# Gate product zs stored raw in a gated attention and gMLP block: silu and factors taken in later pairs, query parts laid out row by row

## The chip, the cores and the metric

The kernel runs on one core of a Trainium2 chip. The metric is the device time of one execution in microseconds (us); the time of a kernel is the median of several executions.

## The reference

One layer of a streaming encoder over 1024 tokens of width 1024, all in float32. Cut to what the change touches:

```python
h = rmsnorm(x, norm_g)
q, k, v, za, u, vs, zs, gm = split(h @ w_in)          # columns of one projection
q, k = partial_rope(q, pos), partial_rope(k, pos)     # first 16 of 64 dims of each head
a = window_sink_attention(q, k, v, sinks)             # 16 heads, 2 key heads, chunks of 64
a = (a * silu(za)) @ w_att_out
sgo = chunked_spatial_gating(gelu(u), gelu(vs), ...)  # called s1 in the kernel
sgo = (sgo * silu(zs)) @ w_sg_out
ga, gs = split(sigmoid(gm + b_merge))
y = ga * a + gs * sgo
out = rmsnorm(x + y @ w_o, final_g)
```

The output has to hold `silu(zs) * s1` in front of `w_sg_out`, wherever silu and product are taken.

## The kernel before, in words

**Pairs.** Every 1024x1024 projection is made in four *pairs* of 128-row blocks (`m` = 0, 2, 4, 6). A pair is one call of `gemm_pair` (L350): seven products by a Strassen-like scheme instead of eight. A product (L333) is 12 matmuls of 128x512, since each float32 operand is split into a high and a low float32r part (`split`, L148: ScalarE casts the high part, VectorE subtracts it from the source) and three of the four partial products are kept, over four blocks of depth. The seven products come in the order b11, t1, t2, b21, t3, b22, t4, by the names of the seven forms of the right operand (tiles `T_b11h`, `T_b11l` and so on, one buffer each). Between the products stand ScalarE copies out of PSUM (L359, L363, L366), VectorE adds (L371, L376, L380), four calls of `finish`, one for each quarter of the pair's result, and a `hook` after each product. The quarter tiles come from a ring of five (`xtile`, L95), the PSUM banks from rings of two per name (`bank`, L83).

**Weights.** `split_next` (L208) splits one weight tile at four places of a pair (tiles `wh`, `wl`, rings of three); the tiles come from DRAM on SyncE's queue one pair ahead. The engines work through their instructions in order; the order of the program is set by a scheduling layer from the order in which the code is written, dependencies, and the explicit ones that `after` (L158) adds.

**Stages.** In this order: head and vs; four pairs of u with the spatial mixing, which writes `s1_dr` (L789); the pair of keys and values; four pairs of q; four pairs of zs; four of gs and four of ga (both merge gates, stored raw by `rest`, L464); four of za; four of `w_sg_out`; four of `w_att_out`; the last projection. The attention runs beside the zs pairs from `m` = 2 on and beside gs and ga: each hook there takes one or two *parts* of the generator `attention` (`part_of_attention`, L1255, nine parts for a pair, one for a hook in the first pair): scores and exponentials (`softmax_stage`, L1097), transposes of the weights (`weight_stage`, L1151), values (`value_stage`, L1183).

**The q pairs.** `finish` (L984) stores a quarter raw to `q_raw` and, scaled and split, to `q_hl`, shape (2, 1024, 1024), high part first (`split_q`, L883, store at L894). The rotary rows go through `rotate` (L937): loads of `q_raw` on SyncE's queue (L943, tiles `rot`), six VectorE operations (L963 to L970), and `split_q` again. `rotate(1, 1)` falls into the first zs pair. `query_stage` (L1032) loads 64x4x128 blocks of `q_hl` for the attention (L1038).

**The zs pairs.** `zs_pair` (L1052) collects the four quarters. When the pair's products are issued, it takes the silu of all four on ScalarE (L1069), after the latest sink exponential (L1138), then multiplies each by its quarter of `s1_dr` on VectorE (L1079) and stores it to `s_dr` (L1080). The factors are loaded by `get` (L459): in the first pair into `rot` tiles after the products, later two of them ahead, into two buffers `g`.

**The za pairs.** `finish` (L1367) takes silu of the quarter, multiplies it by a quarter of `at_dr`, the attention's result (tiles `g`, four buffers, a pair ahead), and stores `a_dr`. From `m` = 2 on, `part_of_loads` loads the four quarters of `s_dr` (`bq`, 128x4x512, 1 MB each, four buffers, L1286). `forms_of` (L1327) makes the seven forms of the next right operand from them, b11 to t4, on ScalarE and VectorE (L155, L156, L185).

## Time and profile before

| what | value |
|---|---|
| time, three runs | 929.25, 927.65, 929.3 us; median 929.25 |
| the profiled execution's own time | 928.08 us |
| its span, first to last instruction | 926.3 us, 1.78 us less |
| mean granted TensorE clock | 0.996 |
| busy TensorE (PE) | 908.1 us, 98% |
| busy VectorE (DVE), ScalarE (ACT), GpSimd (POOL) | 689.6, 529.5, 126.9 us |
| moved by DMA | 201.71 MB, mean 218 GB/s |

Times in the profile count from the start of the span. In a group of instructions stand the line, the engine, the operation, output<-input, shape and count, then busy us and mean ns of one, then the idle time of the engine just before and what ended it. In a timeline a row has start, duration (of the group if several instructions are merged, "x4"), engine, line, operation, and in brackets the idle time ahead of it and its releaser. PE is TensorE's matmul, SPq SyncE's queue of DMA issues. Where matmuls overlap in the records, the distance of two starts is the cost of one: 0.227 us for 128x512. A row of stretches has start:end, length, then busy us and count for PE, PEld (weight loads), DVE, ACT and POOL, then granted clock, share of the DMA engines and GB/s.

### The profile page before, as it was taken

The numbers are of one execution on the slowest core, as the hardware profiler recorded it, in microseconds if no ns is written. First come the engines' busy times: TensorE is split into PE (matmuls) and PEld (weight loads), VectorE is DVE, ScalarE is ACT, GpSimd is POOL, SyncE is SP. The second block draws the span as 40 slices with busy tenths as digits, with TensorE's granted clock in tenths as the row PEclk, the third lists the DMA queues.
The fourth block names the chain that finished last, engine by engine and source line by source line (L and its number), as shares of the span: only waits on it lengthen the run. The fifth ranks groups of instructions, "written<-read, shape, count | busy, mean of one in ns | idle before, by whom it ended". The sixth has DMA issues, their size and how long they took to land.

```text
span 926.3 us, 13212 instructions
## 1 busy us (share of the span) xinstructions
PE 908.1 (98%) x4332; PEld 753.4 (81%) x4332; DVE 689.6 (74%) x1243; ACT 529.5 (57%) x1056; POOL 126.9 (14%) x189
## 2 busy tenths in 40 slices
PE   8999999999999989999999999999999999999996
PEld 5888888888888778888888888888887887888885
DVE  6874776656678678888878888746498589579996
ACT  6862433334444468887766676744475475467443
POOL 0002222213011001101111121001100111210012
PEclk9999999999999999999999999999999999999999
DMA  6327678877788777878787779779658765998632
GB/s 239 137 87 208 212 192 185 167 155 220 238 284 266 214 240 193 220 214 233 188 228 258 234 172 254 213 259 327 214 200 316 266 198 156 295 310 286 205 114 114
DMA packets 128830, 201.71 MB, mean 218 GB/s; under 512 B 12441, under 2 KB 60825, under 8 KB 128762
## 3 DMA queue, kind: packets, MB, share of 16 engines
q1 hardware_dynamic: 109608, 148.17, 48.9%
q0 software_dynamic: 19008, 52.44, 23.7%
q8 instruction: 34, 0.56, 0.2%
q14 instruction: 34, 0.28, 0.1%
q10 hardware_dynamic: 146, 0.27, 0.1%
HBM read 144.07 MB, written 86.11 MB: 249 GB/s over the span
## 4 chain that ended last, share of the span: by engine, by line
PE 83%; DVE 9%; DMA 3%; issue 2%; ACT 2%; SPq 0%; DVEq 0%; ACTq 0%
PE ps_mm L341 34%; PE ps_o L341 25%; PE ps_mm L600 4%; PE ps_sc L1115 3%; PE ps_sc L341 2%; PE ps_tp L341 2%; PE ps_o L1200 2%; PE ps_tp L1159 2%; DVE wl L156 2%; PE ps_tp L772 2%; DVE bq L185 1%; PE ps_tp L569 1%; PE ps_sc L569 1%; PE ps_o L569 1%; PE ps_mm L569 1%
## 5 line engine op out<-in xcount | busy, mean ns | idle before, releaser
L155 ACT CAST wh<-s 128x1024 fp32r<-128x1024 f32 (+1 forms) x78 | 78.2, 1005 | 96.1 <-PE ps_mm L341 43.1
L156 DVE TENSOR_TENSOR wl<-wr,wh 128x1024 fp32r<-128x1024 f32 (+1 forms) x80 | 75.7, 947 | 55.3 <-ACT wh L155 54.6
L155 ACT CAST wh<-wr 128x1024 fp32r<-128x1024 f32 (+1 forms) x80 | 66.3, 830 | 81.8 <-PE ps_mm L341 39.0
L156 DVE TENSOR_TENSOR wl<-s,wh 128x1024 fp32r<-128x1024 f32 (+1 forms) x78 | 90.9, 1166 | 12.1 <-ACT wh L155 12.1
L341 PE MATMUL ps_o<-T_b22h,wh 128*128 128x512 f32 x148 | 59.6, 403 | 2.5 <-ACT x L363 2.5
L341 PE MATMUL ps_o<-T_t1h,wh 128*128 128x512 f32 x148 | 59.3, 400 | 0.3 <-ACT wh L155 0.2
L341 PE MATMUL ps_o<-T_b22l,wh 128*128 128x512 f32 x148 | 58.3, 394 | 0.0
L341 PE MATMUL ps_o<-T_b22h,wl 128*128 128x512 f32 x148 | 58.3, 394 | 0.0
L341 PE MATMUL ps_o<-T_t1h,wl 128*128 128x512 f32 x148 | 57.8, 391 | 0.0
L341 PE MATMUL ps_o<-T_t1l,wh 128*128 128x512 f32 x148 | 57.6, 389 | 0.0
L341 PE MATMUL ps_mm<-T_b11h,wl 128*128 128x512 f32 x140 | 54.8, 392 | 2.0 <-DVE wl L156 2.0
L341 PE MATMUL ps_mm<-T_t4h,wh 128*128 128x512 f32 x140 | 55.2, 394 | 1.5 <-DMA q<-q_hl 0.8
L341 PE MATMUL ps_mm<-T_t2h,wh 128*128 128x512 f32 x140 | 54.9, 392 | 1.2 <-ACT x L359 1.2
L1128 ACT ACTIVATE pr<-ps_sc,sm 128x192 f32<-128x192 f32 (+2 forms) x128 | 50.9, 409 | 8.3 <-DVE sm L1124 7.2
L341 PE MATMUL ps_mm<-T_t3h,wh 128*128 128x512 f32 x140 | 55.2, 395 | 0.0
L341 PE MATMUL ps_mm<-T_b11h,wh 128*128 128x512 f32 x140 | 55.0, 393 | 0.0
L341 PE MATMUL ps_mm<-T_t4h,wl 128*128 128x512 f32 x140 | 54.7, 391 | 0.0
L341 PE MATMUL ps_mm<-T_b11l,wh 128*128 128x512 f32 x140 | 54.7, 390 | 0.0
L341 PE MATMUL ps_mm<-T_t3h,wl 128*128 128x512 f32 x140 | 54.6, 390 | 0.0
L341 PE MATMUL ps_mm<-T_t2h,wl 128*128 128x512 f32 x140 | 54.6, 390 | 0.0
L341 PE MATMUL ps_mm<-T_t2l,wh 128*128 128x512 f32 x140 | 54.5, 390 | 0.0
L341 PE MATMUL ps_mm<-T_t4l,wh 128*128 128x512 f32 x140 | 54.5, 389 | 0.0
(354 smaller groups left out, 2407.8 us busy)
## 6 DMA issues: line engine op xcount, KB each, us to landing
wr<-in_w_dram SPq DMA_DIRECT2D x86, 256.0 KB
sums<-in_w_dram POOLq DMA_DIRECT2D x20, 512.0 KB, 5.7
s<-sums SPq DMA_DIRECT2D x20, 512.0 KB
s_dr<-x SPq DMA_DIRECT2D x32, 256.0 KB
q_hl<-qhl SPq DMA_DIRECT2D x16, 512.0 KB
q<-q_hl SPq DMA_DIRECT2D x64, 128.0 KB
wr<-in_w_dram SPq DMA_DIRECT2D x14, 512.0 KB
y_dr<-x POOLq DMA_DIRECT2D x28, 256.0 KB, 6.6
```

Source lines behind the costliest of these rows:

```text
L155: nc.scalar.copy(hi, src)
L156: return nc.vector.tensor_sub(lo, src, hi.bitcast(F32))
L185: op(dst[:, i : i + 2, :], a[:, i : i + 2, :], c[:, i : i + 2, :])
L341: nc.tensor.matmul(acc, lt, rt, start=fresh and k == 0 and n == 0, stop=k == 3 and n == 2, skip_group_check=True,)
L569: mm = nc.tensor.matmul(acc, lt, rt, start=k == 0 and n == 0, stop=k == KC - 1 and n == 2)
L600: nc.tensor.matmul(acc[:], lt, rt, start=k == 0 and n == 0, stop=k == KC - 1 and n == 2)
L772: nc.tensor.matmul(pm[:, t * P : (t + 1) * P], xh[:, half * 4 + t, g * P : (g + 1) * P], bias[-1][1][:, g % 4, :], start=True, stop=True,)
L1115: nc.tensor.matmul(sc[:, i, k0:], q_of[:, c, i * P : (i + 1) * P], kt[:, f, k0:], start=f == 0, stop=f == 1,)
L1128: nc.scalar.activation(held_in[c, i], sc[:, i, lo:hi], AF.Exp, bias=nmax[:, c, i : i + 1], scale=-1.0, accum_out=sums[:, c, i : i + 1],)
L1159: nc.tensor.transpose(dst, pr[:, i, block * P : block * P + width], ident[:])
L1200: nc.tensor.matmul(po[:, cs], lt, rt, start=n == 0, stop=n == len(terms) - 1)
```

## The change

1. `zs_pair` goes. The zs pairs use `rest` and store the raw quarter to `z_dr` right after each quarter is made: no silu, no factor, no wait for the exponentials.
2. The za pairs get a table of steps by pair and hook (`parts_of_s`): load the quarters of `z_dr` into `bq` tiles (four named buffers now), take silu in them on ScalarE (128x1024 each), load the same quarter of `s1_dr` as factor, and multiply on VectorE (128x1024). The factor uses buffer 0, which the last quarter needs; so that quarter's factor comes in four pieces of 128x512 through tiles `g2` and `g3`.
3. The za pairs' own factors from `at_dr` have two buffers, `g0` and `g1`, instead of four, and are asked for two quarters ahead instead of four.
4. `q_hl` becomes (1024, 2, 2, 512): for each row and half, high and low part beside each other, 4 KB in a piece; a rotated group is stored by two DMAs in place of four.
5. `rotate`'s loads of `q_raw` go to GpSimd's queue.

The diff, cut to its core (`bq(n)` in place of the ring of four and `want_gate` in place of `want_gates` at other places are left out):

```diff
-    q_hl = scratch("q_hl", (2, D, S))
+    q_hl = scratch("q_hl", (D, 2, 2, HALF))
...
         for at, dst in places:
-            nc.sync.dma_start(dst, hl[at].bitcast(F32))
+            nc.sync.dma_start(dst, hl[at].rearrange("p a t -> p (a t)").bitcast(F32))
...
-                nc.sync.dma_start(dst[halves[half]], src[:, :, half_of(half)])
+                nc.gpsimd.dma_start(dst[halves[half]], src[:, :, half_of(half)])
...
-            rows = q_hl[j].rearrange("(c r d) t -> r d c t", r=2, d=HD)[par]
+            rows = q_hl[:, t // 4, j].rearrange("(c r d) t -> r d c t", r=2, d=HD)[par]
...
-    def zs_pair(m, hook, *place, ahead_by=0):
...
-    zs_pair(0, part_of_q, 5, "rot")
+    gemm_pair(hb, rest(z_dr, 0), part_of_q)
...
-        exps.append(nc.scalar.activation(es[:], es[:], AF.Exp))
+        nc.scalar.activation(es[:], es[:], AF.Exp)
...
-    for m in range(2, KC, 2):
-        zs_pair(m, lambda: part_of_attention(m == 2), 2, ahead_by=3)
-    for dst in (gs_dr, ga_dr):
-        for m in range(0, KC, 2):
-            gemm_pair(hb, rest(dst, m), part_of_attention)
+    for dst in (z_dr, gs_dr, ga_dr):
+        for m in range(2 if dst is z_dr else 0, KC, 2):
+            gemm_pair(hb, rest(dst, m), lambda: part_of_attention(dst is z_dr and m == 2))
...
+        def silu(j, half):
+            for c in range(0, 4, 2):
+                v = s_q[j, half][:, c : c + 2, :]
+                nc.scalar.activation(v, v, AF.Silu)
+
+        def multiply(j, half, c):
+            v = s_q[j, half][:, c : c + 2, :]
+            after(nc.vector.tensor_mul(v, v, factors[-1][:, c : c + 2, :]), term[0])
...
+            (0, 1): [(load, 0, 0), (load_factors, 0, 0)],
+            (0, 2): [(load, 0, 1)],
+            (0, 3): [(load, 1, 1)],
+            (0, 5): [(silu, 0, 0)],
+            (0, 6): [(multiply, 0, 0, 0)],
+            (0, 7): [(multiply, 0, 0, 2), (load_factors, 0, 1)],
+            (2, 3): [(silu, 0, 1)],
+            (2, 6): [(multiply, 0, 1, 0)],
+            (2, 7): [(multiply, 0, 1, 2), (load_factors, 1, 1), (silu, 1, 1)],
+            (4, 2): [(multiply, 1, 1, 0), (multiply, 1, 1, 2), (load, 1, 0), (load_last, 0), (load_last, 1)],
+            (4, 6): [(silu, 1, 0)],
+            (4, 7): [(multiply_last, 0), (multiply_last, 1), (load_last, 2), (load_last, 3)],
+            (6, 1): [(multiply_last, 2), (multiply_last, 3)],
...
     for m in range(0, KC, 2):
         if m == 0:
-            want_gates(at_dr, m)
-        if m == 2:
-            s_q = {}
-            ahead_of_time += loads_of_quarters(s_q, s_dr)
+            for _ in range(2):
+                want_gate(at_dr, *of_att.pop(0), 2)
...
-            if m < 6:
-                gates.append(get(at_dr, m + 2 + i, half, 4))
+            if of_att:
+                want_gate(at_dr, *of_att.pop(0), 2)
 
-        gemm_pair(hb, finish, part_of_loads, "tp")
+        gemm_pair(hb, finish, lambda: part_of_s(m), "tp")
```

**Where instructions stand now.** Three places of the two in-order engines that feed TensorE. First VectorE, at the end of the first zs pair and the start of the second, before:

```order
L245 TENSOR_TENSOR s_2588<-wr_2581,s_2587 128x512
L156 TENSOR_TENSOR wl_2721<-s_2587,wh_2720 128x1024
L156 TENSOR_TENSOR wl_2741<-s_2588,wh_2740 128x1024
L1079 TENSOR_TENSOR x_2590<-x_2590,rot_2756 128x512
L1079 TENSOR_TENSOR x_2592<-x_2592,rot_2760 128x512
L1079 TENSOR_TENSOR x_2591<-x_2591,rot_2764 128x512
L1079 TENSOR_TENSOR x_2739<-x_2739,rot_2768 128x512
L156 TENSOR_TENSOR wl_2895<-wr_2582,wh_2894 128x512
L1123 TENSOR_REDUCE sm_2793<-ps_sc_2796 128x2
```

The same place now (L1087 is the first operation of the softmax, L1123 before):

```order
L380 TENSOR_TENSOR x_2587<-x_2587,ps_o_2610 128x512
L156 TENSOR_TENSOR wl_2716<-s_2583,wh_2715 128x1024
L890 SCALAR_TENSOR_TENSOR qhl_2672<-rot_2603,qhl_2672 128x256 x2
L156 TENSOR_TENSOR wl_2738<-s_2584,wh_2737 128x1024
L1087 TENSOR_REDUCE sm_2770<-ps_sc_2773 128x2
L1087 TENSOR_REDUCE sm_2770<-ps_sc_2782 128x2
```

The four products with factors (L1079) no longer stand between the weights' low parts and the first softmax. Second, VectorE a little earlier, in the first zs pair around the rotation of the queries, before:

```order
L371 TENSOR_TENSOR x_2590<-x_2590,ps_o_2656 128x512
L963 TENSOR_TENSOR rot_2608<-rot_2606,tab_306_2068 128x512
L156 TENSOR_TENSOR wl_2671<-wr_2581,wh_2670 128x1024
L964 TENSOR_TENSOR rot_2609<-rot_2607,tab_318_2124 128x512
L969 TENSOR_TENSOR rot_2606<-rot_2606,tab_318_2124 128x512
L965 TENSOR_TENSOR rot_2608<-rot_2608,rot_2609 128x512
L968 TENSOR_TENSOR rot_2607<-rot_2607,tab_306_2068 128x512
L376 TENSOR_TENSOR x_2592<-x_2592,ps_mm_2589 128x512
```

and now:

```order
L960 TENSOR_TENSOR rot_2604<-rot_2602,tab_306_2068 128x512
L371 TENSOR_TENSOR x_2586<-x_2586,ps_o_2650 128x512
L156 TENSOR_TENSOR wl_2666<-wr_2577,wh_2665 128x1024
L961 TENSOR_TENSOR rot_2605<-rot_2603,tab_318_2124 128x512
L966 TENSOR_TENSOR rot_2602<-rot_2602,tab_318_2124 128x512
L962 TENSOR_TENSOR rot_2604<-rot_2604,rot_2605 128x512
L965 TENSOR_TENSOR rot_2603<-rot_2603,tab_306_2068 128x512
L376 TENSOR_TENSOR x_2588<-x_2588,ps_mm_2585 128x512
```

The same eight operations, but L371 now stands behind the first rotation product (L963 before, L960 now). Third, ScalarE in the first za pair, from the copy after product t2 to the copy after b11 of the next pair, before:

```order
L366 COPY x_6316<-ps_mm_6314 128x512
L155 CAST wh_6381<-wr_6293 128x1024
L1368 ACT_TABLE_LOAD
L1368 ACTIVATE x_6315<-x_6315 128x512
L1368 ACTIVATE x_6317<-x_6317 128x512
L155 CAST wh_6421<-s_6295 128x1024
L1368 ACTIVATE x_6316<-x_6316 128x512
L155 CAST wh_6443<-s_6296 128x1024
L1368 ACTIVATE x_6437<-ps_mm_6314 128x512
L359 COPY x_6456<-ps_mm_6455 128x512
```

and now, from the second silu of a quarter of z on (L1349; L1398 is the silu of za, L1368 before):

```order
L1349 ACTIVATE bq_1140_6259<-bq_1140_6259 128x1024
L1398 ACTIVATE x_6245<-x_6245 128x512
L155 CAST wh_6359<-s_6227 128x1024
L1349 ACTIVATE bq_1143_6277<-bq_1143_6277 128x1024
L1398 ACTIVATE x_6244<-x_6244 128x512
L1349 ACTIVATE bq_1143_6277<-bq_1143_6277 128x1024
L1398 ACTIVATE x_6376<-ps_mm_6242 128x512
L155 CAST wh_6382<-s_6228 128x1024
L1349 ACTIVATE bq_1146_6296<-bq_1146_6296 128x1024
L359 COPY x_6398<-ps_mm_6397 128x512
L1349 ACTIVATE bq_1146_6296<-bq_1146_6296 128x1024
```

Of the eight silu on quarters of z, six stand in this one stretch, the first of them just ahead of these rows behind the table load, and five stand ahead of the copy L359; the table of steps has two of the quarters a pair later, the scheduling layer put them here. On SyncE's queue all three quarters and the first factor, 4 MB, are issued in one run between the second and the third of the gates from `at_dr`.

98 lines of the change are left out of this document (51 added, 47 removed).

## The prediction, as put on record before the run

> **What bounds the kernel now.** The head of the page comes first, then TensorE's waits over the whole span (us in total, times, longest):
>
> ```profile
> PE 908.1 (98%) x4332; PEld 753.4 (81%) x4332; DVE 689.6 (74%) x1243; ACT 529.5 (57%) x1056; POOL 126.9 (14%) x189
> ```
>
> ```profile
> PE ps_o L341 <- ACT x L363: 2.5, 1, 2.5
> PE ps_mm L341 <- DVE wl L156: 2.0, 2, 1.1
> ...
> PE ps_mm L341 <- ACT x L359: 1.2, 2, 0.9
> ...
> PE ps_mm L341 <- DVE x L376: 0.7, 1, 0.7
> ```
>
> TensorE is the bound, so only what it loses can be won. Those waits are small, but they don't show how much slower it ran around them. The table of stretches does; first from t1 of the second zs pair to t1 of the first gs pair (four pairs), then four later pairs:
>
> ```profile
> 320.77:432.45 111.68, 107.05 (x556) 88.39 (x556) 91.06 (x215) 85.23 (x228) 11.88 (x14) 0.98 0.80 225
> 458.59:562.00 103.41, 103.41 (x569) 89.29 (x568) 84.15 (x198) 72.59 (x211) 14.10 (x20) 1.00 0.77 222
> ```
>
> The later four run without a gap. Both stretches hold 28 products; by the code the first has 34 parts of attention, the second 36. From the chain, a product takes 2.72 (24 matmuls in 5.44):
>
> ```profile
> 626.62 5.44 PE ps_mm L341 x24
> ```
>
> So 28 products are 76.2, the 36 parts 27.2 or 0.76 each, and the first stretch without its stalls is 103.41 - 2 x 0.76 = 101.9. **It loses 9.8 us**: 4.6 idle (111.68 - 107.05), the rest slower running. The largest piece shows why (timelines of the four engines):
>
> ```profile
> 328.80 0.39 PE L341 MATMUL ps_o<-T_b21h,wl 128*128 128x512 f32 x1
> 331.67 0.80 PE L341 MATMUL ps_o<-T_b22h,wh 128*128 128x512 f32 x1 [2.49 <-ACT x L363]
> ...
> 334.40 0.63 PE L341 MATMUL ps_o<-T_b22h,wh 128*128 128x512 f32 x1
> ```
>
> ```profile
> 314.23 5.13 SPq L894 DMA_DIRECT2D q_hl<-qhl  x8
> ...
> 320.74 1.85 SPq L200 DMA_DIRECT2D rot<-s_dr  x4
> ...
> 328.52 2.50 SPq L457 DMA_DIRECT2D s_dr<-x  x4
> ```
>
> ```profile
> 327.80 0.69 DVE L1079 TENSOR_TENSOR x<-x,rot 128x512 f32<-128x512 f32 x1 [6.79 <-DMA rot<-s_dr]
> ```
>
> ```profile
> 331.02 0.60 ACT L363 ACTIVATE x<-ps_o 128x512 f32<-128x512 f32 x1 [4.12 <-DMA s_dr<-x]
> 331.94 1.28 ACT L1128 ACT_TABLE_LOAD   x1 [0.32 <-DMA s_dr<-x]
> ```
>
> Read it backwards. Product b22 needs L363, which needs one of the five quarter tiles; that is free only when its store is done, and the store waits for the factor, which SyncE issues behind eight stores of `q_hl` (the trace gives the name `s_dr` to loads of `s1_dr` too). VectorE stands 6.79 at the product with the factor. TensorE loses 331.67 - 328.80 - 0.23 = 2.6, and seven matmuls after it cost (334.40 - 331.67) / 6 = 0.46 each instead of 0.23, another 1.6: 4.2 in all.
>
> **The change: zs beside the attention.** These operations leave the four zs pairs:
>
> ```profile
> L1069 ACT ACTIVATE x<-x 128x512 f32<-128x512 f32 x12 | 7.1, 624 | 0.6 <-DVE x L376 0.5
> L1069 ACT ACT_TABLE_LOAD x4 | 5.1, 1283 | 0.1
> L1128 ACT ACT_TABLE_LOAD x4 | 5.1, 1283 | 0.4 <-DMA s_dr<-x 0.3
> ...
> L1079 DVE TENSOR_TENSOR x<-x,g 128x512 f32<-128x512 f32 x12 | 8.2, 690 | 7.3 <-DMA g<-s_dr 3.9 <-ACT x L1069 3.2
> ```
>
> Seven of the eight table loads go (9.0 us of ScalarE), and 16 silu and 16 products. What stays has the same sequence per quarter as gs and ga, whose stretch has no stall, so all 9.8 are to be had. One thing is late next: the first softmax, which now follows TensorE closely. Its scores, then t1 and 9 matmuls of t2, then its transposes: 21 matmuls are 4.8, and the second scores about 1, so 5.8. Before, that chain took
>
> ```profile
> 331.19 0.61 DVE L1123 TENSOR_REDUCE sm<-ps_sc 128x2 f32<-128x128 f32 x2
> ```
>
> ```profile
> 336.55 0.68 PE L1159 MATMUL ps_tp<-ident,pr 128*128 128x128 f32 x4
> ```
>
> 5.4, with a table load in it. The cover is 0.4; ScalarE's L363 and VectorE's weight parts share it. Bounds 0 and 1.5 lost; I take 0.8. **Term: -9.0** (-9.8 to -8.3).
>
> **Rotation in the first zs pair.** The last product of that pair waits for L376:
>
> ```profile
> 305.17 2.56 SPq L943 DMA_DIRECT2D rot<-q_raw  x4
> ```
>
> ```profile
> 309.62 0.69 DVE L963 TENSOR_TENSOR rot<-rot,tab 128x512 f32<-128x512 f32 x1 [0.73 <-DMA rot<-q_raw]
> ...
> 311.61 0.69 DVE L964 TENSOR_TENSOR rot<-rot,tab 128x512 f32<-128x512 f32 x1 [0.16 <-DMA rot<-q_raw]
> ...
> 314.02 0.68 DVE L376 TENSOR_TENSOR x<-x,ps_mm 128x512 f32<-128x512 f32 x1
> ```
>
> This stall (0.7 in the list of waits) does not go: the rotation stays in front of L376. Now L371 (0.6) also waits for the rotation's first load: the rows from 309.62 to 314.02 move down by its 0.6, less the idle 0.16 in them, so L376 comes some 0.4 later. And the four loads come by GpSimd's queue. Not shown before; the nearest rows for that queue (KB each, us from issue to landing):
>
> ```profile
> at_dr<-aT POOLq DMA_DIRECT2D x16, 256.0 KB, 5.4
> ...
> k_dr<-qhl POOLq DMA_DIRECT2D x16, 32.0 KB, 3.3
> ```
>
> Between them for 128 KB; SyncE's took 4.4 to the first rotation (309.62 - 305.17). So 1.1 earlier to 1.0 later; I take no difference, since 4.4 is also the middle of the two rows. Half as many SyncE issues for rotated rows free the queue, nothing waits for that any more. **Term: +0.4** (-0.7 to +1.4).
>
> **The za pairs.** ScalarE gets eight silu of 1024 and VectorE six products of 1024 and four of 512; for their sizes stand a cast and a subtraction, 1.05 and 1.22:
>
> ```profile
> L155 ACT CAST T_b11h<-bq x2: 1050/1052/1053, 670.7 to 671.6; 128x1024 fp32r<-128x1024 f32 x2
> ```
>
> ```profile
> L185 DVE TENSOR_TENSOR bq<-bq,bq 128x1024 f32<-128x1024 f32 x16 | 19.1, 1217 | 0.9 <-DMA bq<-s_dr 0.9
> ```
>
> That is 8.4 and 10.0 us. The room is in the stretches of the first za pair; DVE is the third of the five busy times after the length, ACT the fourth:
>
> ```profile
> 603.00:623.00 20.00, 20.00 (x96) 16.66 (x94) 8.55 (x12) 9.16 (x14) 1.14 (x2) 1.00 0.71 246
> 623.00:643.00 20.00, 20.00 (x89) 16.54 (x89) 12.04 (x16) 8.61 (x13) 2.19 (x4) 1.00 0.99 355
> ```
>
> Both are half idle, so it fits on average. The tight place is the end of the first pair: six silu between 619 and 634, five ahead of L359.
>
> ```profile
> 618.80 0.58 ACT L366 COPY x<-ps_mm 128x512 f32<-128x512 f32 x1
> ...
> 632.10 0.59 ACT L359 COPY x<-ps_mm 128x512 f32<-128x512 f32 x1 [1.36 <-PE ps_mm L341]
> ```
>
> Walking its new order with these durations: table load to 620.7, silu and quarter's silu in turn to 625.2, the weight cast when its buffer is free at 626.5, then three silu of z, two of za, one cast, and L359 ends at 633.3. TensorE needs it for t2 at
>
> ```profile
> 634.78 2.72 PE ps_mm L341 x12
> ```
>
> so 1.4 are left. The last silu ahead of L359 needs quarter (1,1) by 631.7. In front of its end are 0.5 MB of sums, 0.5 of gates and four times 1 MB, 5.2 MB from about 613.3 on: at the 355 GB/s of the lower of these two rows 628.0, at the 246 of the upper 634.6, then late by 2.9, of which 1.4 is covered. I take the higher rate, since a queue with several MB in it is the lower row's case, and 0.2 for the rest. **Term: +0.2** (0 to +1.5).
>
> VectorE's backlog later, when the forms are made, is what the `wl` waits above stand for. The last two products with factors stand ahead of it, in
>
> ```profile
> 671.74 2.36 DVE L156 TENSOR_TENSOR T_b11l<-bq,T_b11h 128x1024 fp32r<-128x1024 f32 x2 [1.56 <-ACT T_b11h L155]
> ```
>
> two times 0.69 in an idle 1.56: nothing, up to 1 if their loads are late. The longer pieces of `q_hl` are hidden: no wait hangs on bytes there.
>
> **Sum.** -9.0 + 0.4 + 0.2 = **-8.4**. The profiled execution took 928.08 (span 926.3 and 1.8 around it), 1.2 below the median shown; it would take 919.7. With the three runs the mean is 928.57, and from there I forecast **920.2**.
>
> **The rivals.** *A, rotation loads late.* GpSimd's issue is held up or its landing slow. For it: nothing but software issue stands there. Against: 3.3 and 5.4 above. If they come 3 later, L376 waits 3 more and TensorE slows after it as at 331.67: 3 + 1.6, so 924.8. In the Trainium skill, "SBUF — State Buffer", section "SBUF: two separate sides", speaks against this edit: while VectorE runs an operation in a two-port mode, GpSimd cannot write the descriptors of its DMAs. By that rule the loads would wait for VectorE, which makes A likelier where such operations run; the trace's k_dr landing of 3.3 beside a working VectorE shows no such hold.
>
> *B, ScalarE waits for z.* At 246 GB/s the first za pair loses 1.5, and the quarters' chain (factor, product, next load into buffer 0) as much again: 923.
>
> *C, the stall only moves.* The first softmax or a quarter tile's store stops TensorE by 2 to 3 as before, and it slows again: 4.2 of the 9.8 stay, 924.4.
>
> *D, slower: gates two quarters ahead.* A gate from `at_dr` is now asked for after the product two places earlier, and VectorE meets it two quarters on, with the weights' low part behind it.
>
> ```profile
> 642.26 0.69 DVE L1369 TENSOR_TENSOR x<-x,g 128x512 f32<-128x512 f32 x1
> ...
> 647.74 0.68 DVE L1369 TENSOR_TENSOR x<-x,g 128x512 f32<-128x512 f32 x1
> ```
>
> That leaves 647.74 - 642.95 = 4.8 to land 256 KB, and TensorE takes the low part about 2 later. A store of that size took 4.75:
>
> ```profile
> 300.35 4.75 DMA q_raw<-x
> ```
>
> so it holds on average. To be slower, the four pairs must lose 10.3 (the 8.4 and 0.2%), 2.6 each: landing 9.4 or more after the issue, every time. Behind the 4 MB that can happen once, not four times. It would give 931.
>
> **Chances.** Forecast 0.62 (917.8 to 922), A 0.12, B 0.14, C 0.05, D 0.07. Faster by over 0.2% of 929.25 (1.9 us, about what a measurement of this kernel can tell from no change) is a time below 927.4: the forecast, A, B and 0.02 of C, together 0.90. Within 0.2% is the rest of C, 0.03, where more of the loss returns than the 4.2 kept there; slower is D, 0.07. The range reaches from the forecast with all bounds good to A and B: 917.8 to 925.5.
>
> **What would show it.** Right: no wait on L363, L359 or `q` between 320 and 432, four pairs in about 102.7; no ACT_TABLE_LOAD at each zs pair any more, only one ahead of the first exponential and one ahead of the first silu of za; L376 at 314 to 315; L359 of the second za pair before 634 by the old clock. Wrong: idle TensorE at the first transposes (C), a `rot` wait over 1.5 on VectorE (A), a ScalarE wait for `bq` (B), a VectorE wait for `g` in every za pair (D).

## The result and the profile after

The changed kernel takes **932.82 us** (median of ten runs, 930.46 to 936.28), the kernel before, beside it, 928.66 (ten runs, 927.65 to 929.3). The ratio is **1.0047** with a 95% interval of 1.0036 to 1.0059: slower, where the forecast was 920.2. The profiled execution of the changed kernel took 931.92 us, its span is 930.1, its mean granted clock 0.992.

The head of the page after:

```profile
PE 908.0 (98%) x4332; PEld 755.4 (81%) x4332; DVE 688.2 (74%) x1237; ACT 519.9 (56%) x1045; POOL 131.7 (14%) x197
```

ScalarE and VectorE have less to do, as forecast, and TensorE the same. The span is 3.8 longer all the same. TensorE's waits over the span (us in total, times, longest) show one new large one:

```profile
PE ps_mm L341 <- DVE x L376: 8.6, 3, 5.0
```

That line had 0.7 in one wait before. To see where the time went, the span is cut at the first matmul of t1 in each pair and each stretch compared with its own before:

| stretch | before | after | difference | forecast |
|---|---|---|---|---|
| pair of keys and values, last 20 us | 20.16 | 20.84 | +0.7 | - |
| first zs pair | 20.94 | 27.75 | **+6.8** | +0.4 |
| the four pairs from the second zs pair to the first gs pair | 111.68 | 102.32 | **-9.4** | -9.0 |
| third za pair | 19.04 | 24.07 | **+5.0** | +0.2 |
| making the forms (second stretch behind it) | 14.90 | 14.90 | 0 | 0 |
| one pair behind 804 | 19.04 | 19.87 | +0.8 | - |

With -0.4 in the head and +0.1 between the ends, that makes +3.7; the spans differ by 3.8. The stretches after; the first two answer to the two of before:

```profile
327.89:430.21 102.32, 102.31 (x556) 87.82 (x556) 81.46 (x201) 72.46 (x215) 11.78 (x14) 1.00 0.70 190
456.39:559.84 103.45, 103.45 (x569) 89.28 (x568) 84.16 (x198) 72.53 (x211) 14.07 (x20) 1.00 0.75 219
648.82:672.89 24.07, 21.01 (x86) 16.75 (x84) 16.57 (x20) 9.52 (x13) 2.15 (x5) 0.93 0.77 270
```

The four pairs now run without a gap at full clock, as the later four do. The third za pair has idle TensorE of 3.1 and a clock of 0.93. So the part of the change that was worked out most closely came true, and two parts that were put down as nearly free cost 11.8.

**The first zs pair after.** Timelines of SyncE's queue, GpSimd, VectorE and TensorE, in that order:

```profile
302.32 0.82 SPq L457 DMA_DIRECT2D q_raw<-x  x1
...
306.34 2.70 SPq L1035 DMA_DIRECT2D q<-q_hl  x4
```

```profile
308.69 1.67 POOL L943 DMA_DIRECT2D rot<-q_raw  x3 [5.91 <-DMA q_raw<-x]
```

```profile
313.26 0.69 DVE L960 TENSOR_TENSOR rot<-rot,tab 128x512 f32<-128x512 f32 x1 [6.36 <-DMA rot<-q_raw]
...
318.44 0.68 DVE L376 TENSOR_TENSOR x<-x,ps_mm 128x512 f32<-128x512 f32 x1
```

```profile
319.17 0.79 PE L341 MATMUL ps_mm<-T_t4h,wh 128*128 128x512 f32 x1 [5.04 <-DVE x L376]
...
323.60 0.63 PE L341 MATMUL ps_mm<-T_t4l,wh 128*128 128x512 f32 x1
```

Three of the four loads are issued at 308.69, when the last store of `q_raw` has landed, some 3 us later than SyncE issued them before (305.17 to 307.73). The four loads of the queries for the attention go out just ahead of them, from 306.34 on. VectorE stands 6.36 at the first rotation, L376 ends at 319.12, and TensorE has lost 5.04. After that the rows are (323.60 - 319.17) / 10 = 0.44 apart instead of 0.23 for a dozen matmuls.

**The third za pair after.** SyncE's queue, VectorE, ScalarE, TensorE:

```profile
650.31 0.37 SPq L200 DMA_DIRECT2D bq<-s_dr  x1
...
662.16 0.37 SPq L200 DMA_DIRECT2D bq<-z_dr  x1
```

```profile
659.77 2.36 DVE L1353 TENSOR_TENSOR bq<-bq,bq 128x1024 f32<-128x1024 f32 x2 [5.48 <-DMA bq<-s_dr]
...
662.65 0.68 DVE L371 TENSOR_TENSOR x<-x,ps_tp 128x512 f32<-128x512 f32 x1
...
664.99 0.68 DVE L376 TENSOR_TENSOR x<-x,ps_mm 128x512 f32<-128x512 f32 x1
```

```profile
667.28 2.01 ACT L1349 ACTIVATE bq<-bq 128x1024 f32<-128x1024 f32 x2 [0.96 <-DMA bq<-z_dr]
```

```profile
665.72 0.74 PE L341 MATMUL ps_mm<-T_t4h,wh 128*128 128x512 f32 x1 [3.06 <-DVE x L376]
...
669.24 0.39 PE L341 MATMUL ps_mm<-T_t4h,wl 128*128 128x512 f32 x1
```

The factor of quarter (1,1) is loaded into buffer 0 (the trace gives it the name `s_dr`). It can be issued only when the product before it has released the buffer, at 650.31, and is there 9.46 later. Its two products stand on VectorE ahead of L371 and L376, which TensorE needs: 3.06 idle, then eight matmuls at (669.24 - 665.72) / 8 = 0.44, another 1.7. That is 4.8 of the 5.0.

### The profile page after: what moved, and what is told of

Its sections match the earlier page's. It is cut to its first block, busy times and chain, and to the rows that moved or that the text cites. A ratio compares the mean times of both kernels' runs of the same rounds, so it can differ in the third digit from the quotient of the medians.

```text
span 930.1 us, 13173 instructions
## 1 busy us (share of the span) xinstructions
PE 908.0 (98%) x4332; PEld 755.4 (81%) x4332; DVE 688.2 (74%) x1237; ACT 519.9 (56%) x1045; POOL 131.7 (14%) x197
## 4 chain that ended last, share of the span: by engine, by line
PE 81%; DVE 8%; DMA 6%; issue 2%; ACT 1%; SPq 0%; POOL 0%; DVEq 0%; ACTq 0%; POOLq 0%
PE ps_mm L341 33%; PE ps_o L341 24%; PE ps_mm L600 5%; PE ps_sc L1079 3%; DMA wr<-in_w_dram 2%; PE ps_o L1164 2%; PE ps_sc L341 2%; PE ps_tp L1123 2%; DVE wl L156 2%; PE ps_tp L341 2%; DVE bq L185 1%; PE ps_tp L569 1%; PE ps_sc L569 1%; PE ps_o L569 1%; PE ps_mm L569 1%
## 5 line engine op out<-in xcount | busy, mean ns | idle before, releaser
L156 DVE TENSOR_TENSOR wl<-wr,wh 128x1024 fp32r<-128x1024 f32 (+1 forms) x80 | 75.6, 946 | 44.6 <-ACT wh L155 44.0
L156 DVE TENSOR_TENSOR wl<-s,wh 128x1024 fp32r<-128x1024 f32 (+1 forms) x78 | 91.0, 1166 | 14.3 <-ACT wh L155 14.3
L341 PE MATMUL ps_mm<-T_t4h,wh 128*128 128x512 f32 x140 | 57.1, 408 | 8.6 <-DVE x L376 8.6
```

Source lines behind the costliest of these rows:

```text
L156: return nc.vector.tensor_sub(lo, src, hi.bitcast(F32))
L341: nc.tensor.matmul(acc, lt, rt, start=fresh and k == 0 and n == 0, stop=k == 3 and n == 2, skip_group_check=True,)
```

## The experiments

All were timed in five rounds beside the kernel before, which took 927.8 to 928.2 in them; ratios are to that kernel. Three figures follow each median: first zs pair / first attention pair / third za pair, from the profiled execution. Before they are 20.94 / 28.55 / 19.04, after the change 27.75 / 24.13 / 24.07.

Each of the three is the length of one stretch in one execution, and they scatter. Eleven of these kernels, the changed one among them, hold the same instructions in the same order on every engine in the za pairs: the third za pair takes 22.09 to 25.84 in them. The first attention pair takes 25.53 and 27.95 in two kernels that are the same there. The first zs pair is steadier: 27.75 and 27.31, 20.62 and 20.23, and 20.60 to 21.62 in groups of kernels that are the same up to its end. So in the second and third figure a difference of 2 or 3 alone shows nothing; where a reading rests on one, the text says so.

### Which of the two edits on the queries' way holds up the first zs pair

My theory from the two traces was the queue: the rotation's loads land late from GpSimd. The rival was the new shape of `q_hl`. Each edit was undone alone, then both.

**Loads back on SyncE's queue.**

```diff
-                nc.gpsimd.dma_start(dst[halves[half]], src[:, :, half_of(half)])
+                nc.sync.dma_start(dst[halves[half]], src[:, :, half_of(half)])
```

> The changed kernel with one line undone: rotate loads q_raw on SyncE's queue again. In the changed kernel the first zs pair lost 6.8 us: VectorE waited 6.36 for the rotated rows, whose loads were issued at 308.69 after a store of q_raw that SyncE issued at 302.32 (300.35 before). Theory queue (the GpSimd queue is the cause: an earlier group's loads stood behind eight writes of k_dr, 265.62 to 270.52, and all that follows on SyncE came later): the store comes 2 us earlier, the wait shrinks below 2, the time falls by 5 to 7 to about 926. Theory layout (stores of q_hl in the new shape land later, so the ring of three split tiles and with it SyncE's queue stands still): the time stays within 2 us of 932.8.

Measured: 929.26, ratio 1.0015 (1.0006 to 1.0024); 24.87 / 25.02 / 24.55. Better by 3.6 than the changed kernel, but the pair stays 3.9 too long.

**Old shape of `q_hl`, loads on GpSimd's queue.**

```diff
-    q_hl = scratch("q_hl", (D, 2, 2, HALF))
+    q_hl = scratch("q_hl", (2, D, S))
...
```

> The changed kernel with q_hl in its old shape, high and low part apart, four stores for a rotated group; loads of q_raw stay on GpSimd's queue. Theory layout: ScalarE's waits for stores of q_hl fall from 13.4 us to about 3, the stall of 6.8 in the first zs pair goes, about 926. Theory queue: the stall stays, within 2 us of 932.8.

Measured: 930.72, 1.0024 (1.0014 to 1.0035); 25.48 / 24.44 / 25.84. So the loads on GpSimd's queue alone cost 4.5 there.

**Both undone**, the edit before this one and

```diff
-                nc.gpsimd.dma_start(dst[halves[half]], src[:, :, half_of(half)])
+                nc.sync.dma_start(dst[halves[half]], src[:, :, half_of(half)])
```

> The changed kernel with both q edits undone; zs raw and za with silu and factors stay. By both theories the 6.8 us of the first zs pair are back to about 0.7 and the time is 925 to 927; the other two losses (5.0 us in the third za pair, 0.9 later) stay. If it is above 930, neither q edit is the cause.

Measured: 927.46, 0.9989 (0.9979 to 0.9999); 20.62 / 27.63 / 23.87. The first zs pair is as before. Each of the two edits alone delays it by 4 to 5, both together by 7. But the first attention pair is 3.5 longer than in the changed kernel: the late first pair had hidden something. That is more than scatter: in the six kernels whose first pair is late (24.87 to 27.75) the next one takes 24.13 to 25.02, in all others 25.39 or more.

**Only the last rotated group's loads on GpSimd's queue**, to tell a slow landing from an earlier group's `k_dr` loads that stand ahead on that queue:

```diff
-                nc.gpsimd.dma_start(dst[halves[half]], src[:, :, half_of(half)])
+                (nc.gpsimd if g else nc.sync).dma_start(dst[halves[half]], src[:, :, half_of(half)])
```

(against the kernel with the old shape)

> The changed kernel with q_hl in its old shape and only the second rotated group's loads (the ones the stall waits for) on GpSimd's queue; the first group's go back to SyncE's. All loads on GpSimd gave 930.7 and a first zs pair of 25.5, none 927.5 and 20.6. Theory k_dr (the first group's loads stand behind eight k_dr writes on GpSimd, and all that follows comes later): about 927.5, first zs pair 20.6 to 21.5. Theory last loads (GpSimd's issue and landing of the second group are slower by themselves): about 930.5, first zs pair near 25.

Measured: 930.84, 1.0027 (1.0018 to 1.0037); 25.22 / 24.83 / 22.59. The last group alone does it. Timelines of SyncE, GpSimd and VectorE in this kernel:

```profile
303.07 3.02 SPq L1038 DMA_DIRECT2D q<-q_hl  x4
```

```profile
304.85 1.69 POOL L943 DMA_DIRECT2D rot<-q_raw  x3 [1.32 <-DMA q_raw<-x]
```

```profile
310.04 0.69 DVE L963 TENSOR_TENSOR rot<-rot,tab 128x512 f32<-128x512 f32 x1 [2.39 <-DMA rot<-q_raw]
...
312.97 0.69 DVE L964 TENSOR_TENSOR rot<-rot,tab 128x512 f32<-128x512 f32 x1 [1.04 <-DMA rot<-q_raw]
```

And in the one with both edits undone, SyncE and VectorE:

```profile
304.62 2.56 SPq L943 DMA_DIRECT2D rot<-q_raw  x4
307.22 0.62 SPq L1038 DMA_DIRECT2D q<-q_hl  x1
...
308.90 1.93 SPq L1038 DMA_DIRECT2D q<-q_hl  x3
```

```profile
309.03 0.69 DVE L963 TENSOR_TENSOR rot<-rot,tab 128x512 f32<-128x512 f32 x1 [0.52 <-DMA rot<-q_raw]
```

This is what "frees the queue" did. On one in-order queue the queries' four loads stood *behind* the rotation's. Freed of those, SyncE issues them at 303.07, beside the rotation's. The first rotation product needs the first two of the four loads. The second is issued at 304.85 here and takes 310.04 - 304.85 = 5.2 to that use; with both edits undone it is issued at 305.34 and takes 309.03 - 305.34 = 3.7. The second use (L964) waits again. Those queries are not needed before the next pair. The Trainium skill, "DMA: Bandwidth & Descriptors", section "Rules for kernel authors", says that spreading DMAs over SyncE, ScalarE and GpSimd gains no bandwidth, because all run on the same 16 DMA engines and interleave; these rows fit that. But no run kept the queries' loads back with the rotation's on GpSimd, so that they are what delays the landing is argued, not shown. The rival is GpSimd's queue itself: from issue to landing its four loads take here

```profile
DMA to landing us min/median/max: 5.1/6.0/6.9
```

and in the changed kernel the first of the four, issued at 302.19, 4.1 before the queries' loads, took 5.5 as well.

### Why the new shape delays it too

The shape has two sides: pieces of 4 KB instead of 2 KB, and two stores for a rotated group instead of four.

**Rotated groups by four stores in the new shape** (loads on SyncE's queue in this and the next three):

```diff
-                        halves[half],
-                        q_hl[:, half].rearrange("(h d) a t -> h d (a t)", h=16)[8 * g : 8 * g + 8, 8 * j : 8 * j + 8],
+                        (halves[half], a),
+                        q_hl[:, half, a].rearrange("(h d) t -> h d t", h=16)[8 * g : 8 * g + 8, 8 * j : 8 * j + 8],
...
```

> The changed kernel with the loads of q_raw on SyncE's queue (929.26; first zs pair 24.87) and q_hl in the new shape, but a rotated group stored by four transfers of 2 KB pieces, as in the old shape. If the two larger rotated stores are what delays the split tiles, the first zs pair goes back to about 20.6; if it is the quarters' stores, it stays near 24.9.

Measured: 927.71, 1.0 (0.9988 to 1.0012); 20.77 / 25.95 / 24.40. The delay is gone, with the quarters still in 4 KB pieces.

**Each quarter by two stores of 2 KB pieces:**

```diff
-            split_q(q[:], [(slice(0, P), q_hl[rows, half].rearrange("p a t -> p (a t)"))])
+            split_q(q[:], [((slice(0, P), a), q_hl[rows, half, a]) for a in range(2)])
```

> The same with the rotated groups by two transfers as changed, but each quarter of q_hl stored by two transfers of 2 KB pieces, high and low part apart. If the quarters' 4 KB pieces are what delays the split tiles, the first zs pair goes from 24.87 to about 20.6; if it is the rotated stores, or if eight more issues on SyncE's queue cost as much, it stays near 24.9 or above.

Measured: 932.92, 1.0056 (1.0041 to 1.0071); 26.79 / 25.00 / 24.01. So the quarters' pieces are not the cause: smaller ones don't help. SyncE's queue with two stores for a rotated group, then with four:

```profile
293.26 1.14 SPq L200 DMA_DIRECT2D wr<-in_w_dram  x1
...
295.61 4.38 SPq L894 DMA_DIRECT2D q_hl<-qhl  x4
...
304.99 2.92 SPq L943 DMA_DIRECT2D rot<-q_raw  x4
```

```profile
294.66 2.99 SPq L897 DMA_DIRECT2D q_hl<-qhl  x5
...
302.83 0.42 SPq L200 DMA_DIRECT2D wr<-in_w_dram  x1
304.90 2.56 SPq L946 DMA_DIRECT2D rot<-q_raw  x4
```

The order differs: with two issues less, the scheduling layer has moved a weight load ahead of five stores of `q_hl` (293.26; it stands at 302.83 in the other) and, before that, the second of the two key loads (both are issued from 282.43 on; it stands at 290.08 in the other). The rotation's loads go out at the same time in both, 304.99 and 304.90, but their first use on VectorE comes 1.0 later with two stores, and the next one (L961) waits another 0.78:

```profile
310.55 0.69 DVE L960 TENSOR_TENSOR rot<-rot,tab 128x512 f32<-128x512 f32 x1 [2.26 <-DMA rot<-q_raw]
```

```profile
309.55 0.69 DVE L964 TENSOR_TENSOR rot<-rot,tab 128x512 f32<-128x512 f32 x1 [0.55 <-DMA rot<-q_raw]
```

So the theory became: the *order* that follows from the number of issues costs the 4 us, not bytes. It can be tried by holding the moved transfers back in the program's order.

**The weight load held behind the last store of `q_raw`:**

```diff
+            seen.append(move)
+            if len(seen) in HELD:
+                after(move, hold[HELD[len(seen)]])
...
```

> The changed kernel with the loads of q_raw on SyncE's queue (929.26; first zs pair 24.87, with four rotated stores 20.77 and 927.71), with one weight load held behind the last store of q_raw by an explicit order, where it stands with four rotated stores; the two rotated stores stay as changed. Theory order (the transfers that moved ahead of the stores are the cause): the first zs pair goes to 20.8 to 22, about 927.5. Theory size (two stores of 4 KB pieces land later by themselves): it stays at 24 to 25, about 929.3.

Measured: 931.15, 1.003 (1.0018 to 1.0042); 21.77 / 26.56 / 22.09.

**And the key loads held behind a store of `q_raw`:**

```diff
-    HELD = {4: -1}
+    HELD = {4: -1, 5: 0}
```

> The same with the two loads of keys held as well, behind the first store of q_raw of the last q pair, so that no load stands ahead of the rotated stores. Theory order: 20.8 to 21.5 in the first zs pair if the weight load alone wasn't enough, about 927.5. Theory size: 24 to 25 again.

Measured: 931.53, 1.0034 (1.0023 to 1.0045); 19.93 / 32.55 / 24.10. For the first zs pair the order theory holds in the one profiled execution of each: 24.87, then 21.77, then 19.93, shorter than before. How the order delays the landing is not shown. And the time does not follow: with the weight load held, the profiled execution took 928.84 but the median is 931.15, and where the other executions lose is not known. With the keys held too, the pair behind loses more. The keys are not late for it (issued from 293.72 on, first scores at 318.33); the first softmax is, since its first tile waits for a store of `q_hl`. VectorE, then TensorE:

```profile
328.00 0.62 DVE L1094 TENSOR_REDUCE sm<-ps_sc 128x2 f32<-128x128 f32 x2 [6.44 <-DMA q_hl<-qhl]
```

```profile
330.88 1.81 PE L1086 MATMUL ps_sc<-k,q 128*128 128x128 f32 x8 [4.35 <-ACT pr L1099]
```

### What the late first pair had hidden

With the first zs pair on time, TensorE waits at the second scores. VectorE, ScalarE and TensorE with both edits undone:

```profile
322.62 0.62 DVE L1092 TENSOR_REDUCE sm<-ps_sc 128x2 f32<-128x128 f32 x2 [2.30 <-DMA z_dr<-x]
```

```profile
323.54 1.28 ACT L1097 ACT_TABLE_LOAD   x1 [3.56 <-DVE sm L1093]
```

```profile
325.58 1.54 PE L1084 MATMUL ps_sc<-k,q 128*128 128x128 f32 x8 [1.62 <-ACT pr L1097]
```

This is rival C: the first softmax is late. Two links of that chain can be taken away: the table load, and the wait of 2.30 of its first tile (`sm`) for a store.

**Table loaded early**, by an exponential of a constant:

```diff
+    warm = const.tile([P, 1], F32, name="warm")
+    nc.gpsimd.memset(warm[:], 0.0)
...
+    after(nc.scalar.activation(warm[:], warm[:], AF.Exp), pace[0])
```

> The changed kernel with both q edits undone, and one exponential of a 128x1 constant on ScalarE behind the first zs pair, so that the table is loaded ahead of the first softmax (the constant's result is used nowhere). With both edits undone the first attention pair takes 27.6 instead of 24.1, with TensorE 1.62 idle at the second scores, since the first softmax waits 2.3 for a store and then 1.28 for its table. Theory first softmax: that idle time falls by 1.28 to about 0.3 and the slow matmuls behind it go, 2 to 3 less in all, about 925. Rival: the stores alone set it and the pair stays above 27.

Measured: 926.0, 0.998 (0.9968 to 0.9993); 20.95 / 25.48 / 24.62. The pair is 2.2 shorter, the median 1.5 lower. The gain is not clear of the noise: the two intervals overlap (0.9979 to 0.9999 without it), and in the six later kernels with the early table the pair takes 25.39 to 27.95.

**First `sm` and `pr` tiles in other memory**, on top of that (the rings `rot` and `wide` shrink to make room):

```diff
-        return mtile(shape, dt, tag, bufs, pool)
+        return mtile(shape, dt, tag, bufs, aheads if tag in ('sm',) else pool)
...
```

> The kernel with both q edits undone and the exponential ahead (926.0, first attention pair 25.48), with the first softmax's scratch (its sums, and its first weights tile pr) in memory that the closed stage of the queries didn't use; two rings of that stage are a buffer or two shorter for it. So the first softmax no longer waits until the last stores of q_hl have landed. Theory memory (that wait is what makes the first attention pair late): VectorE's first reduction comes about 2 us earlier, TensorE's 1.05 at the second scores goes, the pair falls to 24.1 to 24.4 and the time to about 924.7. Rival: VectorE's own work in front of it (the weights' low parts) keeps the reduction where it is, and the pair stays above 25.

Measured: 927.33, 0.9986 (0.9977 to 0.9995); 20.37 / 25.53 / 24.54. VectorE's wait is gone, and TensorE waits later in the pair for something else:

```profile
320.64 0.28 DVE L1097 TENSOR_REDUCE sm<-ps_sc 128x2 f32<-128x128 f32 x1
```

```profile
331.71 1.20 PE L1089 MATMUL ps_sc<-k,q 128*128 128x256 f32 x8 [1.33 <-DMA q<-q_hl]
```

The pair is no shorter (25.53 against 25.48), nor is the time: the wait of 2.30 was real, and taking it away brought no gain that shows.

**The kernel before with the first zs pair's factors on GpSimd's queue.** This tests my reading of before itself, that the factor behind eight stores makes the 4.2:

```diff
+            nc.gpsimd.dma_start(g[:], s1_dr[(m + i) * P : (m + i + 1) * P, half_of(half)])
...
```

> The kernel before with only the four factor loads of the first zs pair moved from SyncE's queue, where they stand behind eight stores of q_hl, to GpSimd's queue. By the prediction's reading of the largest stall (4.2 us at 329 to 334: store behind product behind factor behind those stores) the factors land 4 us or more earlier and the stall goes: 924 to 925. If the first softmax or the table loads are late anyway, another stall takes its place and the time stays within 1.5 us of 928.2.

Measured: 930.46, 1.0029 (1.0019 to 1.0039); 22.07 / 29.33. TensorE's wait for L363 makes way for one at the second scores, VectorE's row ahead of it:

```profile
326.82 0.62 DVE L1128 TENSOR_REDUCE sm<-ps_sc 128x2 f32<-128x128 f32 x2 [2.81 <-DMA s_dr<-x]
```

```profile
329.78 1.39 PE L1120 MATMUL ps_sc<-k,q 128*128 128x128 f32 x8 [3.32 <-ACT pr L1133]
```

The largest stall of before can be moved without any gain: two chains end close together there.

### The third za pair

The theory: product (1,1) waits for its factor, and L371 behind it on VectorE. The rival: the loads of the quarters are late as a chain, so that one removal only shows the next wait.

**The product (1,1) later, behind L371 and L376, and all that follows it later too:**

```diff
-            (4, 2): [(multiply, 1, 1, 0), (multiply, 1, 1, 2), (load, 1, 0), (load_last, 0), (load_last, 1)],
-            (4, 6): [(silu, 1, 0)],
+            (4, 6): [(multiply, 1, 1, 0)],
+            (4, 7): [(multiply, 1, 1, 2), (load, 1, 0), (load_last, 0), (load_last, 1)],
+            (6, 3): [(silu, 1, 0)],
...
```

> The changed kernel with the product of the third quarter (1,1) with its factor moved from after t1 to after b22 and t4 of the third za pair, and what follows it (load of the last quarter, its factors, silu and products) moved by as much. In the changed kernel VectorE waited 5.48 us for that factor ahead of the add L371, and TensorE lost 5.0 us there. If that order is the cause, the wait on L376 in that pair goes and the time falls by 4 to 5 to about 928; if the factor load itself is too late for any place, VectorE waits there again, or the forms of the next operand come late (over 1 us at about 704), and the time falls by less than 2.

Measured: 936.58, 1.0092 (1.0079 to 1.0105); 27.31 / 24.32 / 19.17. The third pair is whole; the fourth takes 25.31, because ScalarE stands at the last quarter's silu ahead of its copy L366 (TensorE waits 3.14 for that), and the next stages lose 4.3 more:

```profile
676.76 1.06 ACT L1349 ACTIVATE bq<-bq 128x1024 f32<-128x1024 f32 x1 [4.48 <-DMA bq<-z_dr]
```

**The factor of (1,1) in four pieces through `g2` and `g3`, earlier** (on the kernel with both edits undone):

```diff
+            (2, 1): [(load_piece, 1, 1, 0), (load_piece, 1, 1, 1)],
+            (2, 4): [(multiply_piece, 1, 1, 0), (multiply_piece, 1, 1, 1), (load_piece, 1, 1, 2), (load_piece, 1, 1, 3)],
...
```

> The changed kernel with both q edits undone (927.46 measured), and the factors of quarter (1,1) taken in four pieces of 128x512 through g2 and g3, as the last quarter's are, from the second za pair on; buffer 0 then carries one load less and the last quarter's load starts after the second product instead of the third. Theory chain (each 1 MB load through buffer 0 takes about 9 us and the third is waited for ahead of L371): the third za pair goes from 23.9 back to 19.04 and the time falls by 4 to 5, to about 923. Theory bytes (the za pairs move 4 MB more and are short of bandwidth wherever the loads stand): a wait of 3 us or more stays or comes back elsewhere, and the time falls by less than 2.

Measured: 932.38, 1.0047 (1.0031 to 1.0063); 20.23 / 27.63 / 20.56. The third pair loses only 1.5, the second, fourth and the forms lose 4.1, 1.3 and 1.7 instead. The wait stands at the pieces now:

```profile
639.92 0.69 DVE L1365 TENSOR_TENSOR bq<-bq,g 128x512 f32<-128x512 f32 x1 [3.52 <-DMA g<-s_dr]
```

**Both products (0,1) and the load behind them earlier** (on the kernel with the table early, as the next three):

```diff
-            (2, 6): [(multiply, 0, 1, 0)],
-            (2, 7): [(multiply, 0, 1, 2), (load_factors, 1, 1), (silu, 1, 1)],
+            (2, 5): [(multiply, 0, 1, 0), (multiply, 0, 1, 2), (load_factors, 1, 1)],
+            (2, 7): [(silu, 1, 1)],
```

> The same kernel (926.0) with both products of the second quarter (0,1) with its factor moved up to behind L376 of the second za pair, and the load of the third factor, which follows them in buffer 0, with them: it is issued at about 644 by the changed kernel's clock, 6 earlier. Theory chain (the third factor is late because its load starts late): it lands before L371 of the third za pair, which goes from 24.6 to 19.0 or 19.5, about 921. Theory bytes (each of these loads takes 8 to 10 us because the queues are full wherever they stand): the second factor is not there at L376, the loss moves to the second za pair or stays, and the time falls by less than 2.

Measured: 930.99, 1.0031 (1.0019 to 1.0043); 20.60 / 25.55 / 26.37. The factor is there earlier, and then ScalarE waits for the last quarter of z in front of a silu of za that VectorE needs:

```profile
647.65 2.36 DVE L1361 TENSOR_TENSOR bq<-bq,bq 128x1024 f32<-128x1024 f32 x2 [2.81 <-DMA bq<-s_dr]
...
659.27 0.69 DVE L1407 TENSOR_TENSOR x<-x,g 128x512 f32<-128x512 f32 x1 [5.79 <-ACT x L1406]
```

```profile
657.66 1.06 ACT L1357 ACTIVATE bq<-bq 128x1024 f32<-128x1024 f32 x1 [5.99 <-DMA bq<-z_dr]
```

**That one load of 1 MB left out:**

```diff
+            if (j, half) == (1, 1):
+                return
```

> The same kernel (926.0) with the load of the third quarter's factors left out: the product of quarter (1,1) takes the second quarter's factors that still stand in the buffer. If the wait for that one load is the whole loss of the third za pair, the pair goes from 24.6 to 19.04 and the time falls by about 5.5, to 920.5. If the last quarter's own load and silu are late as well, some 1 to 3 us of it come back in that pair or the next.

Measured: 928.06, 1.0006 (0.999 to 1.0021); 21.62 / 25.77 / 23.07. Without the transfer that I had named as the cause, the pair still loses 4.0, and the fourth and the forms 1.3 and 2.0. The profiled execution took 932.15, more than the median, but the median is no lower than the 926.0 either: the theory of one late factor falls. ScalarE's wait at the silu of the last quarter takes over, whose load of 1 MB was issued at 648.51 (the row names a weight load, the one that ended last by the profile):

```profile
656.45 1.06 ACT L1359 ACTIVATE bq<-bq 128x1024 f32<-128x1024 f32 x1 [3.75 <-DMA wr<-in_w_dram]
```

**The earlier products and the tiles in other memory together:**

```diff
+            (2, 5): [(multiply, 0, 1, 0), (multiply, 0, 1, 2), (load_factors, 1, 1)],
...
+        return mtile(shape, dt, tag, bufs, aheads if tag in ('sm',) else pool)
```

> Both q edits undone, the exponential ahead, the first softmax's scratch apart, and the second quarter's products with the third factor's load moved up: the last two edits together. By the theories memory and chain 924.7 less 4 to 5, about 920; by their rivals about 925.

Measured: 930.91, 1.0025 (1.0009 to 1.0041); 20.51 / 27.95 / 24.55. No better than either.

**All factor loads but the first left out** (3 MB):

```diff
+            if factors:
+                return
...
-            (4, 7): [(multiply_last, 0), (multiply_last, 1), (load_last, 2), (load_last, 3)],
-            (6, 1): [(multiply_last, 2), (multiply_last, 3)],
```

> Both q edits undone and the exponential ahead (926.0; third za pair 24.6), with the factor loads left out but the first: the second and third quarter are multiplied by the first's factors, the last by none. The four loads of z, their silu and the products of three quarters stay; 3 MB less are loaded. If the factors are the whole cause, the third za pair goes to 19.04 with no loss in the pairs behind it, about 920.5. If the loads of z and the silu in the za pairs are too much by themselves, 2 us or more stay.

Measured: 921.48, 0.9935 (0.9921 to 0.9948); 20.25 / 25.39 / 19.91. The stretch of the third za pair with the factors, then without:

```profile
643.30:667.92 24.62, 21.05 (x85) 16.78 (x84) 16.78 (x20) 9.51 (x13) 2.21 (x5) 0.93 0.78 264
```

```profile
642.12:662.03 19.91, 19.34 (x86) 15.69 (x84) 13.88 (x16) 9.63 (x13) 2.16 (x4) 1.00 0.70 234
```

The factors are 4.7 of the 5.6 lost, and 4.5 of the median; 19.91 lies well outside the 22.09 to 25.84 above. VectorE's busy time falls by only 2.9, so most of it is waiting. The DMA engines are 0.78 busy at 264 GB/s, below the 0.99 and 355 of the second of the two stretches before: the mean rate alone doesn't set it. Whether it is the time that a load takes beside the others or the chain of loads through one buffer isn't separated, since this run removes both.

**Two of the four zs pairs the old way**, so that only two quarters need silu and factor in za:

```diff
+    gemm_pair(hb, rest(z_dr, 2), lambda: part_of_attention(True))
+    for m in range(4, KC, 2):
+        zs_pair(m, part_of_attention, 2, ahead_by=3)
...
-            (2, 7): [(multiply, 0, 1, 2), (load_factors, 1, 1), (silu, 1, 1)],
+            (2, 7): [(multiply, 0, 1, 2), (load, 1, 0)],
...
```

> Both q edits undone, the exponential ahead; the zs pairs of the first two column blocks (m = 0, 2) raw as in the change, those of m = 4, 6 with silu and factor beside the attention as in the kernel before, so the za pairs make two quarters and only load the other two. Theory factors: the za pairs lose nothing (4 x 19.04), the two zs pairs lose 1.5 to 2 each again (table loads and factors, 27.5 to 28 instead of 26.15): 926.0 - 5.5 + 3.5, about 924. Rival: the chain of the first two quarters alone, or the late load of the last, still stops a za pair by 2 or more: 926 or above.

Measured: **923.45**, 0.9959 (0.9944 to 0.9975); 20.63 / 27.16 / 19.04. This beats both kernels. The za pairs lose nothing, the two zs pairs lose 4.1 against raw stores (56.39 - 52.28). The stretches: third za pair and last two zs pairs of this kernel, then the two zs pairs with raw stores:

```profile
647.76:666.80 19.04, 19.04 (x85) 15.77 (x84) 13.75 (x16) 7.63 (x11) 2.16 (x4) 1.00 0.85 276
372.78:429.17 56.39, 53.89 (x292) 45.01 (x290) 47.63 (x105) 45.70 (x115) 8.31 (x10) 1.00 0.87 227
```

```profile
372.49:424.77 52.28, 52.28 (x291) 45.20 (x290) 43.06 (x100) 37.25 (x107) 8.31 (x10) 1.00 0.77 199
```

## Why the prediction was wrong

**zs beside the attention, -9.0: right in size, on borrowed cover.** The four pairs went from 111.68 to 102.32, -9.4, and the table loads went as counted; one each is left:

```profile
L1092 ACT ACT_TABLE_LOAD x1 | 1.3, 1283 | 2.8 <-DVE sm L1088 2.8
L1349 ACT ACT_TABLE_LOAD x1 | 1.3, 1283 | 2.6 <-DMA bq<-z_dr 2.6
```

But with the first zs pair on time the same four pairs take 105.72 (both edits undone), a gain of only 6.0. The rest came from the first pair's lateness, in which loads and the first softmax caught up. Two terms were added as if independent; they were not. The late first softmax, for which the term held 0.8, was then worth up to 3.4 (105.72 - 102.32; 1.8 in the kernel with four rotated stores, whose four pairs took 104.14).

**Rotation in the first zs pair, +0.4 (-0.7 to +1.4): failed, +6.8.** The failing step is "Half as many SyncE issues for rotated rows free the queue, nothing waits for that any more". I costed the moved loads by their own landing time, took the time of their issue as given, and did not ask what SyncE would issue in their place. In the changed kernel L376 starts at 318.44, 4.4 later than before, where 314 to 315 was the sign of being right. Of this 2.8 is the issue: the second load, which the first product needs, goes out at 308.69 instead of 305.89, because the last store of `q_raw` is issued at 302.32 instead of 300.35 and lands only then. Another 0.8 is its landing (4.6 to the first use instead of 3.7), and 0.6 is L371 in front, which the term had. TensorE then loses 4.3 more idle time and 2.6 in slow matmuls. Two things changed in the queues: the queries' loads move ahead and run beside the rotation's; and with two stores less the scheduling layer orders SyncE's queue anew. That each edit alone costs this much is shown: 4.9 for the loads (20.62 to 25.48), 4.3 for the shape (20.62 to 24.87), both together 7.1. How each of them delays the landing stays open. Rival A had the right symptom, a `rot` wait of 6.36 on VectorE, and a cause that was only part of it; its 4.6 was too small. The hold of GpSimd's issue that the Trainium skill's rule under rival A speaks of is not seen: in the kernel with the second group on GpSimd three issues take 1.69, 0.56 each, also in the 0.69 of it in which VectorE works (L156 from 305.57 on). Whether that operation is of the kind which the rule means, no row shows.

**The za pairs, +0.2 (0 to +1.5): failed, +5.0.** The first pair was walked step by step, and there it was right: the copy L359 of the second za pair ended at 631.34, by the old clock at 633.5 (the stage starts 2.12 earlier now), and the walk has 633.3. The loss came two pairs later, in steps that I did not walk: the third and fourth loads into buffer 0. Rival B named that chain and gave it 1.5; it is 4.8, since a load of 1 MB takes 9.46 there and the products behind it stand ahead of L371 and L376. That load is not the whole cause: without it 4.0 are still lost, without the 3 MB of later factors 0.9. No single move or split there takes the loss away; fewer quarters do. Whether it is the bytes or the chain through one buffer stays open.

**Forms, 0:** right. **Rival D:** a single VectorE wait for `g` of 1.92, not one in every pair.

**The sum.** With the first pair on time, the change is worth -6.0 in the four pairs, -0.3 in the first and +4.8 in the third za pair, -1.5; the kernel with both edits undone measured 927.46, -1.0 by its ratio. The two query edits then cost 932.82 - 927.46 = 5.4. The rivals A and B had been treated as alternatives. A came, and of B the chain (its first pair lost nothing); A and the whole of B together would have given 927.6 by their own prices, which were too low as well. The lower end of the range is off by 0.3: with all bounds good the sum is 928.57 - 9.8 - 0.7 = 918.1, not 917.8. The small losses in the keys' pair (+0.7) and behind 804 (+0.8) were not followed; the second is there, 0.3 to 1.3, in every kernel with the new za pairs, and in neither of the two with the old ones.

## What to carry to other kernels

An in-order DMA queue also works as a schedule: before taking a transfer off it, look at what will be issued in its place, and whether that will run beside something that the critical engine needs. Where work is moved into a stage with spare engine time, walk the last link of the chain of loads through its buffers, not the first. And add gains only after asking whether one stall is the cover of the next; undoing each part alone and then both shows it. Before a stretch of one profile decides between two theories, see how much it scatters in kernels that are the same there.

## What the runs showed of the hardware that was not expected

- A load of 1 MB took 9.46 from issue to first use (650.31 to 659.77), and 5.12 a little later (662.16 to 667.28). The DMA engines moved 284 and 264 GB/s in those two stretches, at a share of 0.83 and 0.75. From rate and length, some 2.7 MB went through in the first and 1.35 MB in the second (an estimate), so the other transfers beside the load make the difference, not the rate.
- After the waits of 2.49, 3.06 and 5.04 us shown above TensorE ran seven to a dozen matmuls at 0.43 to 0.46 us instead of 0.23. The Trainium skill, "TensorE: Matmul & The Clock Gate", section "Why this matters for your kernels", warns of gaps above about 3 us; the gap of 2.49 before the change already cost seven slow matmuls. Nor does a longer gap always cost them: in the third za pair a gap of 2.12 was followed by eight (the kernel without one factor, at 659.40), one of 3.10 by none (the last rotated group on GpSimd, at 663.52), one of 2.76 by none (the weight load held, at 661.10). That is part of the scatter of that pair.
- The first tile of a stage waits for the last stores of the closed stage whose memory it takes: 2.30, 2.81 and 6.44 in the rows of `sm` above. In other memory (the kernel with `sm` and `pr` moved) the wait is gone.
